# Moving work within the beginnings of two ConvFFN layers, and four smaller moves around them

## The chip, the cores and the metric

The kernel runs on one core of a Trainium2 chip. The metric is the device time of one execution in microseconds (us). Times of a kernel are medians of several executions; the trace is of one execution taken by the hardware profiler. The engines are PE (TensorE, matrix products), PEld (its weight loads), DVE (VectorE), ACT (ScalarE), POOL (GpSimd) and SP (SyncE, which issues DMAs). Each engine works through its own list of instructions in order, and waits on semaphores for the others.

## The reference

A two-layer sequence encoder over x of 1 x 1024 x 1024 in float32. Both layers add a mixing block and a gated convolutional FFN to the residual h, each behind an RMSNorm:

```python
for layer in range(2):
    if layer == 0:
        h = h + gated_deltanet(rmsnorm(h, a_norm[0]), ...)
    else:
        kv = rmsnorm(h, kv_norm) @ w_kv            # keys and values, once
        h = h + chunk_attention(rmsnorm(h, b_norm[0]), w_q, rel_bias, w_out, kv)
    h = h + conv_ffn(rmsnorm(h, f_norm[layer]), ...)
return rmsnorm(h, final_norm)

def gated_deltanet(xn, ...):
    ...                                            # causal conv, SiLU, chunked delta rule: o
    o = rmsnorm(o, out_norm_w) * silu(z)
    return o @ w_out

def conv_ffn(xn, w_up, conv_w, conv_b, w_down):
    h = causal_dwconv(xn @ w_up, conv_w) + conv_b  # three taps along the sequence
    gate, val = h[..., :2816], h[..., 2816:]
    return (silu(gate) * val) @ w_down
```

The model width is 1024, the sequence 1024 long, the FFN 2 x 2816 wide. Attention has 16 heads of 64 over bands of nine chunks of 64 with a relative bias.

## The kernel before

**Products.** Every large product is done in three passes: both operands are cut into a high part (a rounding to the type fp32r, on ACT) and a low part (operand less high part, on DVE or POOL), and PE multiplies high by high, low by high and high by low. `triple` (and `dense` outside the FFN) issues such three matmuls of 128x128 by 128x512. One activation tile is 128 channels by 1024 positions, worked on in two halves of 512.

**Stages in order.** The gated DeltaNet (layer 0's mixing, about the first 668 us), FFN layer 0, the seam in which h is normed for attention and the first K and Q tiles are made (`two_tiles`, near 1310 to 1350), attention, its output product (`queue_out`), FFN layer 1 (from about 1888), the final norm.

**The order of the work.** In the DeltaNet and in attention, a planner written in the kernel (`Weave`, and `Flow` on top of it) calls generators. Each yields the time at which it wants to go on; the planner keeps estimated engine times (`wv.on("A", 0.62)` books 0.62 on ACT) and lays the instructions out from them. `wv.late` is a list of generators that go on when a slot has been reached. In the FFN the order is a list written out by hand: `step` adds a product of 12 matmuls to `seq`, and `at(i, f, rank)` adds the vector work `f` to step i; within a step, jobs run by rising rank. Where the order isn't given by hand (the vector engines in attention, everything in `two_tiles`), the framework's scheduler sets it.

**The FFN.** Both products use a seven-product scheme on 2x2 blocks. The up-projection of the pair j (one `gate` and one `val` tile of 128 channels) takes products (j, n), n from 1 to 7; pair 0 is done in plain by eight steps. For each product the operand is a combination `r` of weight blocks, cut into `uh` (ACT) and `ul` (POOL, in the beginning partly DVE). When a product is done, `after(j, n)` combines its PSUM bank `pu` with `keep` into the pre-activations `vpre` and `gpre`. `taps(j, v, i)` applies tap i of the convolution (v = 1 for `val`, 0 for `gate`; tap 0 with the bias on ACT, L1553; taps 1 and 2 on DVE, L1556), `silu` runs on ACT (L1559), `gated` multiplies on DVE. The down-projection takes two pairs at a time: group g has second products ("d", g, n) with weight operands `dh`, `dl` from `a`, `ay` and activation operands `eh`, `el` from `val`, into banks `pd`, which `drain` copies or adds into `stage` tiles and `send` sends to DRAM. The `when` table says at which step and rank the taps, SiLU and multiply of each pair stand. Helper lines seen in the profile: L1428 is every DVE and POOL addition or subtraction in the FFN, L1449 every rounding on ACT, L1461 to L1463 the three matmuls of `triple`, L1786 the copies of `drain`.

**Norms at the seams.** `norm_steps` sums squares (`nacc`, L401 and L409), sums over partitions with eight tiny matmuls into `pss` (L412), takes the square root (ACT) and reciprocal `rsn` (DVE, L415), broadcasts it with matmuls into `psb` (L425), multiplies h by it (L430, L432) and cuts the result (`xh`, `xl`, L421). It is a generator; the caller places its two sets of matmuls among its own by `next(tail)`. In `two_tiles` and in `plain` of FFN layer 1 these places are given by a pair (i, k): product i, triple k. In `queue_out`, `rest(0)` is put into `wv.late` with `t0 + 11`.

**The other two places.** `yz(k, s)` at the end of the DeltaNet loads y and z tiles, waits until `wv.T + 5.0`, and computes y * SiLU(z) (L1115), which `split_yt` cuts. `split_act` cuts the attention's outputs into `xh` (ACT) and `xl` (L381, even k on DVE, odd k on POOL).

Of the kernel before, what the change touches and what calls it, by code (L numbers as in the profile page):

```python
# [28 lines left out]
def trunk_kernel(  # L29
# [348 lines left out]

    def split_act(dst, src, s, k):
        nc.scalar.copy(dst[0][k][s], src)  # L380
        (nc.vector if k % 2 == 0 else nc.gpsimd).tensor_tensor(dst[1][k][s], src, dst[0][k][s].bitcast(F32), op=ALU.subtract)  # L381

    rsn = const.tile([P, 2, 8], F32, name="rsn")

# [57 lines left out]
    def queue_out(w, h, n, soon, d_r, residual, early, start_need, late_need, g, alloc, begin, begin_need, both, delay, own, ahead):  # L442
# [69 lines left out]
        def rest(s):  # L512
            w_ = 1024 // (KT - n)
            it = norm_steps(h, s, g, normed, keep=True)
            for c in range(KT - n):
                if s == 0:
                    hold.append(load_w(w, c * w_, k0=n, nk=KT - n, w=w_, into=own()))
                wt = hold[c]
                for m in range(c * w_ // P, (c + 1) * w_ // P):
                    ps = alloc()  # L520
                    dense(ps, wt, m * P - c * w_, *acts, [(k - n, k) for k in range(n, KT)], s)
                    yield
                    nc.vector.tensor_tensor(h[m][:, hs(s)], ps, h[m][:, hs(s)], op=ALU.add)
                    nc.scalar.dma_start(out=quarter(d_r, m, s), in_=h[m][:, hs(s)])
                    next(it)

            if s == 1:
                tails.append(it)
                return

            def go():
                t0 = wv.now
                next(it)
                yield
                wv.late.append((lambda: True, lambda: t0 + 3, it))

            t0 = wv.now
            wv.late.append((lambda: True, lambda: t0 + 11, go()))

        tails, hold = [], []  # L540
        acts, normed = [[[[None, None] for _ in range(KT)] for _ in range(2)] for _ in range(2)]
# [29 lines left out]
    with ExitStack() as ph:  # L571
# [535 lines left out]
        def yz(k, s):  # L1107

            yield from wait(("turned", k, s), ("z", k, s))
            yt = yield from take()  # L1110
            nc.sync.dma_start(out=yt, in_=d_y[k][s])
            zt = yield from take()
            nc.sync.dma_start(out=zt, in_=d_z[k][s])
            yield wv.T + 5.0
            nc.scalar.activation(zt, zt, AF.Silu)  # L1115
            yield wv.on("A", 0.62) - wv.slack
            nc.vector.tensor_tensor(yt, yt, zt, op=ALU.mult)
            room.append(zt)
            yield wv.on("D", 0.85) - wv.slack
            yield from wait(("acts", s))  # L1120
            yield from split_yt(yt, s, k)
            room.append(yt)
# [280 lines left out]
    def two_tiles(wts, tail):  # L1403

        pss = [[pacc.tile([P, HALF], F32, name="acc", tag="u", bufs=4) for _ in range(2)] for _ in wts]
        for s in range(2):
            for n, (ps, wt) in enumerate(zip(pss, wts)):
                for i in range(KT):
                    dense(ps[s], wt, 0, xh, xl, FULL[i : i + 1], s, first=i == 0, last=i == KT - 1)
                    if (n, i) in ((0, 6), (1, 3)):  # L1410
                        next(tail, None)
            for _ in tail:
                pass
            yield pss
# [8 lines left out]
    def ffn(layer, h, hp, xs, tail, d_r, last):  # L1423
# [19 lines left out]
        def at(i, f, rank=1):  # L1443

            jobs.setdefault(max(i, 0), []).append((rank, f))
# [169 lines left out]
        def plain(i):  # L1615
            def f():
                s, r, c = ((0, 0, 0), (0, 0, 1), (0, 1, 0), (0, 1, 1), (1, 0, 0), (1, 1, 0), (1, 0, 1), (1, 1, 1))[i]
                if c == 0:
                    first_ps[s, r] = pacc.tile([P, HALF], F32, name="pu0", tag="u", bufs=4)
                if i == 4:  # L1620
                    X[3] = own(hi4, 1)
                x_ = own((lo4, hi4)[c], s)
                for k in range(4):
                    triple(first_ps[s, r], ops0[r, c], x_[k], kc[k], c == 0 and k == 0, c == 1 and k == 3)
                    if (i, k) == ((0, 3), (1, 3))[layer]:
                        next(tail)
                    if (i, k) == ((1, 1), (2, 2))[layer]:
                        for _ in tail:
                            pass
            return f  # L1630
# [8 lines left out]
        for c, (j, n) in enumerate(plan):  # L1639
# [1 line left out]
            due[len(seq)] = (j, n)  # L1641
            step((j, -n), lambda j=j, n=n: product(j, n))
            for g in range(NG):
                for n, o in zip(ORDER, (2, 3, 5, 6, 8, 9, 11) if g == 0 else (-2, 0, 2, 4, 6, 8, 10)):
                    if c == 7 * (2 * g + 1) + 6 + o:
                        step(("d", g, n), lambda g=g, n=n: second(g, n))
        end, fin_at = pos[FP - 1, 7], pos["d", NG - 1, 4]
        early = pos["p", 1, 3]
        for i, (j, n) in due.items():
# [8 lines left out]
                if j > 3 and n in (6, 4):  # L1658
                    at(i - 2, lambda j=j, n=n: left_sum(j, n - 1), 1.05)
            if n != 2 or j > 2:  # L1660
                at(i + 1, lambda j=j, n=n: after(j, n), 0)

        def nx(j, s):
            return pos[j + 1, s] if j + 1 < FP else end + s
# [24 lines left out]
        for j in range(3, FP - 1):  # L1689
# [2 lines left out]

        v0, v1, v2, g0, g1, g2 = [(v, i) for v in (1, 0) for i in range(3)]
        when = {
            0: [(11, (g0,), 0), (12, (v0,), 0), (13, (v1,), 2), (13, (v2,), 2.7), (15, (g1, g2, silu), 2), (17, (gated,), 2)],
            1: [(18, (v0, v1), 2), (19, (v2, g0), 2), (20, (g1,), 2), (21, (g2, silu), 2), (22, (gated,), 2)],
            2: [(24, (v0, v1), 2), (25, (v2, g0), 2), (26, (g1,), 2), (27, (g2, silu), 2), (28, (gated,), 2)],
        }
        for j in range(3, FP - 1):
            late_ = 1 if j == FP - 2 else 0  # L1700
# [722 lines left out]
```

## Time and profile before

| | |
|---|---|
| Time, three executions | 2567.0, 2568.01, 2568.25 us (median 2568.01) |
| Profiled execution | 2567.06 us, its span 2565.4 us |
| PE busy | 2502.9 us (98%), 13933 matmuls |
| DVE / ACT / POOL busy | 1856.2 / 1416.0 / 1468.9 us |
| HBM traffic | 126 GB/s over the span |

The span runs from the first to the last instruction of the profile; about 1.7 us of the execution lie around it. Busy shares are averages over all stages. In rows of the timeline the columns are the start and the duration in us, engine, line, operation, output and inputs with their shape, the count of instructions taken together, and in brackets the idle time before and what ended it. In lists of waits they are total us, times and the longest. In windows the granted clock of PE stands as a share of full speed behind the engines' busy times, then the DMA share and GB/s.

### The profile page before, as it was taken

What the parts mean: (1) busy time and instruction counts of PE and PEld (TensorE: products, weight loads), DVE (VectorE), ACT (ScalarE), POOL (GpSimd) and SP (SyncE); (2) the same over time, 40 slices, a digit from 0 to 9 for tenths busy, and PEclk for the clock granted to TensorE, in tenths of its full rate; (3) what the DMA queues carried; (4) which work ended last, traced back from release to release, by engine and by line L of the source; (5) the groups of instructions that cost most, each with busy time, mean ns of one, the idle gap of its engine ahead of it and who ended that gap; (6) DMA issues with size and microseconds to landing.
All of it is one profiled execution on the core that took longest, in us unless ns stands there. A gap on an engine that the chain in (4) does not pass through costs nothing.

```text
span 2565.4 us, 39382 instructions
## 1 busy us (share of the span) xinstructions
PE 2502.9 (98%) x13933; PEld 2070.2 (81%) x13933; DVE 1856.2 (72%) x3103; ACT 1416.0 (55%) x2736; POOL 1468.9 (57%) x1466
## 2 busy tenths in 40 slices
PE   7999999999999999999999999999999999999998
PEld 5878888888877888888778888887876788888877
DVE  5775874554688888888876666666488788888886
ACT  6444555474455655565555565565455655556544
POOL 3655553445347777777736444443433777777770
PEclk9999999999999999999999999999999999999999
DMA  4533445555337777777932111113332467677795
GB/s 128 137 110 114 128 124 152 147 176 159 101 86 145 147 146 155 155 145 159 204 124 63 54 55 54 52 47 97 107 95 78 135 145 150 143 155 154 152 190 201
DMA packets 320598, 325.15 MB, mean 127 GB/s; under 512 B 32912, under 2 KB 244624, under 8 KB 320400
## 3 DMA queue, kind: packets, MB, share of 16 engines
q1 hardware_dynamic: 289440, 219.33, 28.9%
q0 software_dynamic: 25920, 94.38, 20.8%
q10 hardware_dynamic: 5040, 8.91, 1.0%
q8 instruction: 110, 1.80, 0.3%
q14 instruction: 88, 0.72, 0.1%
HBM read 179.89 MB, written 142.67 MB: 126 GB/s over the span
## 4 chain that ended last, share of the span: by engine, by line
PE 55%; DVE 6%; POOL 4%; issue 3%; ACT 2%; DMA 0%; ACTq 0%; POOLq 0%; DVEq 0%
PE pu L1463 8%; PE pu L1462 8%; PE pu L1461 8%; PE pd L1463 4%; PE pd L1461 4%; PE pd L1462 4%; PE acc L119 3%; PE acc L120 3%; PE acc L121 3%; POOL ul L1428 2%; PE ptp L2139 2%; PE poT L2169 1%; PE sc L2111 1%; PE poT L2168 1%; PE sc L2112 1%
## 5 line engine op out<-in xcount | busy, mean ns | idle before, releaser
L1428 POOL TENSOR_TENSOR ul<-r,uh 128x512 fp32r<-128x512 f32 x282 | 443.0, 1591 | 303.3 <-ACT uh L1449 289.1
L119 PE MATMUL acc<-xh,whi 128*128 128x512 f32 x896 | 373.3, 417 | 1.9 <-DVE kq L686 1.6
L120 PE MATMUL acc<-xl,whi 128*128 128x512 f32 x896 | 353.5, 394 | 1.6 <-POOL xl L421 1.0
L121 PE MATMUL acc<-xh,wlo 128*128 128x512 f32 x896 | 352.8, 394 | 1.1 <-POOL wlo L104 1.1
L1449 ACT CAST uh<-r 128x512 fp32r<-128x512 f32 x296 | 181.7, 623 | 218.4 <-DVE r L1428 169.0
L104 POOL TENSOR_TENSOR wlo<-wraw,whi 128x256 fp32r<-128x256 f32 (+2 forms) x206 | 170.1, 855 | 144.7 <-ACT whi L102 120.7
L1461 PE MATMUL pu<-xh,uh 128*128 128x512 f32 x552 | 216.3, 392 | 1.5 <-DVE h L1329 0.9
L1463 PE MATMUL pu<-xh,ul 128*128 128x512 f32 x552 | 216.1, 391 | 1.1 <-POOL ul L1428 1.0
L1462 PE MATMUL pu<-xl,uh 128*128 128x512 f32 x552 | 215.9, 391 | 1.0 <-POOL xl L421 1.0
L1786 ACT COPY stage<-pd 128x1024 f32<-128x1024 f32 x180 | 174.8, 1013 | 49.2 <-PE pd L1463 49.2
L121 PEld LDWEIGHTS acc<-xh,wlo 128*128 128x128 f32 x896 | 168.7, 188 | 38.7 <-POOL wlo L104 1.6
L120 PEld LDWEIGHTS acc<-xl,whi 128*128 128x128 f32 x896 | 170.1, 190 | 25.7 <-POOL xl L421 3.1
L119 PEld LDWEIGHTS acc<-xh,whi 128*128 128x128 f32 x896 | 169.7, 189 | 24.2 <-DVE kq L686 2.0
L2119 POOL TENSOR_SCALAR sS<-sS,st 128x640 f32<-128x640 f32 (+4 forms) x128 | 85.2, 668 | 171.7 <-DVE st L2118 127.5
L1556 DVE SCALAR_TENSOR_TENSOR val<-vpre,colt,val 128x1023 f32<-128x1023 f32 (+2 forms) x92 | 150.5, 1636 | 40.5 <-ACT val L1553 40.4
L1428 POOL TENSOR_TENSOR dl<-a,dh 128x512 fp32r<-128x512 f32 x90 | 154.8, 1720 | 38.5 <-ACT dh L1449 38.5
L1556 DVE SCALAR_TENSOR_TENSOR gate<-gpre,colt,gate 128x1023 f32<-128x1023 f32 (+2 forms) x92 | 173.0, 1881 | 0.8
L1428 DVE TENSOR_TENSOR r<-r,r 128x512 f32<-128x512 f32 x168 | 133.8, 797 | 29.3 <-POOL ul L1428 28.0
L2117 ACT ACTIVATE sS<-sS,st 128x640 f32<-128x640 f32 (+4 forms) x128 | 89.3, 697 | 100.9 <-DVE st L2116 98.8
L1463 PEld LDWEIGHTS pu<-xh,ul 128*128 128x128 f32 x552 | 104.1, 189 | 24.6 <-POOL ul L1428 3.2
L1461 PEld LDWEIGHTS pu<-xh,uh 128*128 128x128 f32 x552 | 104.1, 189 | 23.6 <-issue 1.3
L1462 PEld LDWEIGHTS pu<-xl,uh 128*128 128x128 f32 x552 | 104.1, 189 | 23.5 <-POOL xl L421 2.1
(405 smaller groups left out, 7146.6 us busy)
## 6 DMA issues: line engine op xcount, KB each, us to landing
r<-in_f_w_up_dram SPq DMA_DIRECT2D x176, 256.0 KB, 4.4
d_r<-stage POOLq DMA_DIRECT2D x78, 512.0 KB, 7.6
d_c<-stage POOLq DMA_DIRECT2D x70, 512.0 KB, 8.0
a<-in_f_w_down_dram SPq DMA_DIRECT2D x72, 256.0 KB, 3.0
wraw<-in_a_w_in_dram SPq DMA_DIRECT2D x32, 512.0 KB, 4.5
d_e<-stage POOLq DMA_DIRECT2D x32, 512.0 KB, 8.8
wraw<-in_a_w_out_dram SPq DMA_DIRECT2D x16, 512.0 KB, 4.3
d_r<-h ACTq DMA_DIRECT2D x32, 256.0 KB, 3.7
```

Of the source, the lines that this page charges most:

```text
L104: nc.gpsimd.tensor_tensor(lo[:, c], raw[:, c], hi[:, c].bitcast(F32), op=ALU.subtract)
L119: mm(ps, hi[:, kw, wcol : wcol + P], rh[k][s], start=st, stop=False)
L120: mm(ps, hi[:, kw, wcol : wcol + P], rl[k][s], start=False, stop=False)
L121: mm(ps, lo[:, kw, wcol : wcol + P], rh[k][s], start=False, stop=sp)
L1428: tt = lambda eng, o, a, b, op: eng.tensor_tensor(o, a, b, op=op)
L1449: copy(hi, src)
L1461: mm(ps, w[0][:, cw], x[0], start=first, stop=False, skip_group_check=True)
L1462: mm(ps, w[0][:, cw], x[1], start=False, stop=False, skip_group_check=True)
L1463: mm(ps, w[1][:, cw], x[0], start=False, stop=last, skip_group_check=True)
L1556: nc.vector.scalar_tensor_tensor(t_[:, a:c1], p_[:, a - step : c1 - step], w[:, 2 - step : 3 - step], t_[:, a:c1], op0=ALU.mult, op1=ALU.add)
L1786: nc.scalar.copy(t_, ps)
L2117: nc.scalar.activation(S, S, AF.Exp, bias=st[:, 1:2], accum_out=st[:, 2:3])
```

## The change

Five groups of edits:

- `split_act`: the low parts of k below 6 all on DVE (before, odd k on POOL).
- `queue_out`: `rest(0)` goes on at slot `t0 + 12` instead of `t0 + 11`.
- `yz`: the wait behind the loads is 8.0 instead of 5.0 of the planner's us.
- The places of the norm's matmuls: in `two_tiles` (1, 1) and (1, 5) instead of (0, 6) and (1, 3); in `plain` of FFN layer 1 (2, 1) and (2, 3) instead of (1, 3) and (2, 2).
- FFN, both layers: the seven second products of group 0 stand at offsets 2, 4, 6, 7, 9, 10, 11 instead of 2, 3, 5, 6, 8, 9, 11, in the order n = 1, 2, 5, 3, 6, 7, 4. In steps: 24, 27, 30, 32, 35, 37, 39 instead of 24, 26, 29, 31, 34, 36, 39. The products (3, 5), (3, 4), (3, 3), (4, 7) and (4, 6) stand one step earlier for it; the rest stay. In `when`, the taps of pairs 0, 1 and 2 are spread, SiLU stands in a step of its own at rank 1.6, and `gated` comes later. `after(3, 2)` stands two steps behind its product instead of one.

```diff
 def split_act(dst, src, s, k):
     nc.scalar.copy(dst[0][k][s], src)
-    (nc.vector if k % 2 == 0 else nc.gpsimd).tensor_tensor(dst[1][k][s], ...)
+    (nc.vector if k % 2 == 0 or k < 6 else nc.gpsimd).tensor_tensor(dst[1][k][s], ...)
...
-            wv.late.append((lambda: True, lambda: t0 + 11, go()))
+            wv.late.append((lambda: True, lambda: t0 + 12, go()))
...
-            yield wv.T + 5.0
+            yield wv.T + 8.0
             nc.scalar.activation(zt, zt, AF.Silu)
...
-                    if (n, i) in ((0, 6), (1, 3)):
+                    if (n, i) in ((1, 1), (1, 5)):
                         next(tail, None)
...
-                    if (i, k) == ((0, 3), (1, 3))[layer]:
+                    if (i, k) == ((0, 3), (2, 1))[layer]:
                         next(tail)
-                    if (i, k) == ((1, 1), (2, 2))[layer]:
+                    if (i, k) == ((1, 1), (2, 3))[layer]:
                         for _ in tail:
                             pass
...
-                for n, o in zip(ORDER, (2, 3, 5, 6, 8, 9, 11) if g == 0 else (-2, 0, 2, 4, 6, 8, 10)):
+                for n, o in zip(ORDER, (2, 4, 6, 7, 9, 10, 11) if g == 0 else (-2, 0, 2, 4, 6, 8, 10)):
...
-                at(i + 1, lambda j=j, n=n: after(j, n), 0)
+                at(i + (2 if (j, n) == (3, 2) else 1), lambda j=j, n=n: after(j, n), 0)
...
-            0: [(11, (g0,), 0), (12, (v0,), 0), (13, (v1,), 2), (13, (v2,), 2.7), (15, (g1, g2, silu), 2), (17, (gated,), 2)],
-            1: [(18, (v0, v1), 2), (19, (v2, g0), 2), (20, (g1,), 2), (21, (g2, silu), 2), (22, (gated,), 2)],
-            2: [(24, (v0, v1), 2), (25, (v2, g0), 2), (26, (g1,), 2), (27, (g2, silu), 2), (28, (gated,), 2)],
+            0: [(11, (g0,), 0), (12, (v0,), 0), (13, (v1,), 2), (13, (v2,), 2.7), (15, (g1,), 2), (16, (g2,), 2), (17, (silu,), 1.6), (19, (gated,), 1.9)],
+            1: [(18, (v0,), 2), (19, (v1,), 2), (19, (v2, g0), 2.1), (21, (g1,), 2), (22, (g2,), 2), (23, (silu,), 1.6), (24, (gated,), 1.1)],
+            2: [(24, (v0, v1), 2), (25, (v2, g0), 2), (27, (g1,), 2), (29, (g2,), 2), (30, (silu,), 1.6), (31, (gated,), 1.9)],
```

More of the change, by code (lines that the diff above doesn't have):

```diff
@@ L380, in split_act @@
         nc.scalar.copy(dst[0][k][s], src)
-        (nc.vector if k % 2 == 0 else nc.gpsimd).tensor_tensor(dst[1][k][s], src, dst[0][k][s].bitcast(F32), op=ALU.subtract)
+        (nc.vector if k % 2 == 0 or k < 6 else nc.gpsimd).tensor_tensor(dst[1][k][s], src, dst[0][k][s].bitcast(F32), op=ALU.subtract)
     rsn = const.tile([P, 2, 8], F32, name="rsn")
```

## The prediction

> **What bounds the kernel now.** I read the page's busy times first, then the waits of PE, then windows over the stretches that the change touches, then the timeline around each wait. Three views carry the argument: the busy line, the waits of PE, and the windows.
>
> ```profile
> PE 2502.9 (98%) x13933; PEld 2070.2 (81%) x13933; DVE 1856.2 (72%) x3103; ACT 1416.0 (55%) x2736; POOL 1468.9 (57%) x1466
> ...
> PE pu L1463 <- POOL ul L1428: 9.7, 17, 1.7
> PE sc L2111 <- DVE st L2115: 6.5, 8, 2.3
> PE pm L939 <- ACT X L932: 2.9, 1, 2.9
> PE pss L412 <- DVE nacc L409: 2.6, 3, 1.4
> ...
> PE pu L1462 <- POOL xl L421: 1.0, 2, 0.7
> ```
> ```profile
> 711.21:781.20 69.99, 64.23 (x269) 49.23 (x268) 58.00 (x59) 37.42 (x52) 38.30 (x26) 1.00 0.34 91
> ...
> 1931.00:2001.00 70.00, 64.48 (x264) 49.48 (x264) 56.40 (x64) 37.84 (x54) 29.08 (x20) 0.98 0.24 79
> ...
> 1000.00:1070.00 70.00, 69.95 (x309) 57.61 (x308) 59.16 (x58) 41.46 (x60) 53.09 (x41) 1.00 0.74 151
> ...
> 551.40:554.70 3.30, 3.30 (x22) 2.97 (x22) 2.70 (x5) 2.79 (x7) 1.78 (x2) 0.50 0.75 251
> 1753.00:1756.00 3.00, 3.00 (x10) 2.32 (x9) 1.53 (x6) 2.05 (x6) 2.05 (x2) 0.50 0.50 151
> 1896.20:1899.50 3.30, 3.30 (x9) 2.63 (x10) 0.20 (x1) 0.74 (x2) 0.11 (x1) 0.50 0.84 235
> 1950.80:1954.10 3.30, 3.30 (x9) 2.55 (x9) 1.68 (x1) 0.05 (x1) 2.89 (x2) 0.50 0.01 3
> ```
>
> PE is busy 98% of the span: 62.5 us of it (2565.4 less 2502.9) are idle, and only PE time can be won. The windows' columns are the stretch, its length, busy time and instructions of PE, PEld, DVE, ACT, POOL, then the granted clock. In the steady FFN stretch (1000 to 1070) PE starts 309 matmuls in 70 us, one every 0.2265 us. In the first seventy us of the two FFN layers, where the down-projection's first group sets in, it starts 269 and 264: 40 and 45 fewer, so 9.1 and 10.2 us of each stretch are lost to idle time, restarts and clock. And four stretches of about 3.4 us run at a granted clock of 0.50: matmuls there are twice as long, so each costs about 1.7 us, after PE had stood idle. In layer 0 the equal stall of 1.74 us left the clock at full speed, so a stall of this size decides it only by where it lies.
>
> **The change, part by part.** Its own time is 2567.06 us (span 2565.4 and 1.66 around it); the median of the runs shown, 2568.01, is 0.95 above it. I sum against 2567.06 and add 0.95 at the end.
>
> *A-layer tail: the gated `z` tiles wait 8.0 instead of 5.0 before SiLU.*
>
> ```profile
> 547.69 0.63 ACT L1115 ACTIVATE spare<-spare 128x512 f32<-128x512 f32 x1 [3.04 <-DMA spare<-d_z]
> 548.34 0.74 ACT L932 COPY X<-pm 32x256 f32<-32x256 f32 x2
> ...
> 549.13 0.21 PE L939 MATMUL pm<-X,D 32*32 32x32 f32 x1 [2.95 <-ACT X L932]
> ...
> PE pu L1461 <- DVE h L1329: 0.9, 1, 0.9
> ...
> PE pu L970 <- DVE vv L847: 0.3, 1, 0.3
> ```
>
> ACT stood 3.04 us in front of a SiLU whose `z` was still on its way from DRAM, with the two copies behind it that PE waited for: 2.95 us idle. The order of the changed program has these copies ahead of that SiLU. The wait goes (2.95), and with it most likely the half-clock stretch at 551 (1.7): 4.6 at best. Against it, the planner lays the rest of the tail out anew (dense products move into the solve, SiLU and its multiply come later), and the later `z` tiles have less room before the output product that reads them; the waits left elsewhere between 480 and 700 are 0.3 to 0.9 each, so a new one costs up to 0.9; with the clock still lost and the stall replaced by four of them, it would end near +1. Range −4.6 to +1; I take −3.5, near the row whose wait is directly undone.
>
> *Attention's end: the first six low parts all on DVE.*
>
> ```profile
> 1746.15 0.42 DVE L2056 CAST qA<-qA 64x512 fp32r<-64x512 f32 x1
> ...
> 1746.94 1.68 DVE L381 TENSOR_TENSOR xl<-eo,xh 128x512 fp32r<-128x512 f32 x1
> ...
> 1749.36 1.51 DVE L2056 CAST qA<-qA 64x512 fp32r<-64x512 f32 x1
> ...
> 1752.25 0.68 DVE L381 TENSOR_TENSOR xl<-eo,xh 128x512 fp32r<-128x512 f32 x1
> ...
> 1746.79 1.29 POOL L381 TENSOR_TENSOR xl<-eo,xh 128x512 fp32r<-128x512 f32 x1 [0.81 <-ACT xh L380]
> 1748.37 2.22 POOL L104 TENSOR_TENSOR wlo<-wraw,whi 128x896 fp32r<-128x896 f32 x1 [0.29 <-ACT whi L102]
> ...
> 1752.13 0.42 PE L2111 MATMUL sc<-kA,qA 128*128 128x320 f32 x1 [2.33 <-DVE st L2115]
> ```
>
> PE waits 2.33 us for the row maximum on DVE, which was late because its subtraction took 1.68 beside POOL's 1.29 (alone 0.68, at 1752.25), and its cast 1.51 beside POOL's 2.22 (alone 0.42, at 1746.15). Without POOL's subtraction the first is 1.0 shorter, so up to 1.0 of the 2.33 goes, and perhaps the half clock behind it (1.7). The three POOL subtractions of each half, 1.29 each, become 0.68 each on DVE: 4.1 us more on an engine that PE waits for here, less about 2.1 of contention. Range −4 to +2; I take −1.5, since the weight-cutting 2.22 stays.
>
> *Norm tail, one slot later (12 for 11).* From 1860 to 1906 PE's waits for `nacc` are these two:
>
> ```profile
> PE pss L412 <- DVE nacc L409: 2.0, 2, 1.4
> ```
>
> 1.37 of it belong to the FFN seam below, the other 0.6 to this tail. A slot is longer, so it goes; the tail then has a slot less to hide. −0.5 (−0.6 to +0.3).
>
> *FFN layer 1's seam: the sums' product moves from after (1,3) to after (2,1), the broadcast from (2,2) to (2,3).*
>
> ```profile
> 1893.61 1.57 DVE L409 TENSOR_TENSOR nacc<-nacc,spare 128x512 f32<-128x512 f32 x1
> ...
> 1895.24 1.06 PE L412 MATMUL pss<-ones,nacc 128*128 128x2 f32 x8 [1.37 <-DVE nacc L409]
> ...
> 1900.98 4.04 DVE L432 SCALAR_TENSOR_TENSOR h<-h,colt,psb 128x512 f32<-128x512 f32 x6 [4.14 <-PE psb L425]
> ```
>
> Six matmuls now stand ahead of `pss`: 6 × 0.2265 = 1.36 us, against 1.37 idle. That wait goes, and with it perhaps the half clock at 1896 (1.7). Six matmuls, not nine, lie between `pss` and the broadcast, so DVE's six `h` products begin 2.4 us earlier if the clock holds and 1.2 if not; PE, 3.1 or 1.4 earlier, then waits up to 0.7 more for the `xl` behind them (the 1.0 of the waits above). Range −2.4 to −1.1; I take −1.8.
>
> *Seam of the two first attention tiles: broadcast from the place behind (1,3) to (1,5), sums from (0,6) to (1,1).*
>
> ```profile
> 1335.40 0.61 PE L425 MATMUL psb<-ident,rsn 128*128 128x128 f32 x4
> ...
> 1337.02 0.61 PE L425 MATMUL psb<-ident,rsn 128*128 128x128 f32 x4
> ...
> 1337.66 1.89 DVE L430 TENSOR_TENSOR nt<-psb,h 128x512 f32<-128x512 f32 x3 [2.77 <-PE psb L425]
> ```
>
> This stretch is ordered by the scheduler, not by hand: in the changed order `pss` lies where it lay, so that half does nothing, and all of `psb` lies five matmuls later (5 × 0.2265 = 1.13). DVE stood 2.77 for it, and PE waits behind DVE and POOL at the end of this seam already. No PE wait that it removes is in the trace. +1.2 (0 to +1.4).
>
> *FFN, both layers: first tiles' taps one per step, SiLU behind the roundings, second products of group 0 two steps apart.*
>
> ```profile
> 715.59 3.50 DVE L1556 SCALAR_TENSOR_TENSOR gate<-gpre,colt,gate 128x1023 f32<-128x1023 f32 x2
> ...
> 753.99 2.59 DVE L1556 SCALAR_TENSOR_TENSOR gate<-gpre,colt,gate 128x1023 f32<-128x1023 f32 x2
> ...
> 716.42 1.28 ACT L1559 ACT_TABLE_LOAD   x1
> 719.11 1.06 ACT L1559 ACTIVATE gate<-gate 128x1024 f32<-128x1024 f32 x1 [1.41 <-DVE gate L1556]
> 720.08 0.60 ACT L1449 CAST uh<-r 128x512 fp32r<-128x512 f32 x1
> ...
> 716.48 1.52 POOL L1428 TENSOR_TENSOR ul<-r,uh 128x512 fp32r<-128x512 f32 x1 [35.60 <-ACT uh L1449]
> 720.81 3.58 POOL L1428 TENSOR_TENSOR ul<-r,uh 128x512 fp32r<-128x512 f32 x2 [2.81 <-DMA r<-in_f_w_up_dram]
> ...
> 723.20 0.50 PE L1463 MATMUL pu<-xt2h,ul 128*128 128x512 f32 x1 [1.74 <-POOL ul L1428]
> ```
>
> The page names a DMA before POOL's 720.81, but what came last is ACT's rounding of 720.08, which stood behind the SiLU of 719.11, which stood 1.41 for a gate tap. With SiLU two steps later the rounding can go 1.41 + 1.06 = 2.5 us earlier, and the 1.74 us stall on `ul` closes: about −2 a layer with the slow restart. In layer 1 the half clock at 1950 follows the same stall (−1.7 if it goes). One step more for five of the second products gives their operands 2.72 us (12 × 0.2265) more, and the remaining 7 us of each layer's 9.1 and more could shrink: I put −5 a layer as the optimistic end. Against it, what is moved later comes due with something else: the table load of 1.28 now stands right in front of the first SiLU, behind which uh for step 20 waits (0.8 by my hand schedule); the multiply of tile 0 and tile 1's taps stand ahead of the weight sums of step 22 (1.5); SiLU of tile 2 at step 30 stands ahead of two drains and a rounding (2 at each of steps 33 and 34), and at step 39 the stage sum stands behind a tap (1.9). These are estimates by hand: the jobs of each step laid end to end at the rows' durations (1.3 a tap, 0.60 a rounding, 1.52 an `ul`, 1.06 a SiLU), DVE and POOL never at the same time. So laid out, it ends at +1.3 a layer: won by step 33, lost by 39. A DVE tap beside POOL took 3.50 for two, 2.59 without, so they do share, but not always. I take −2 in layer 0 and −3 in layer 1 (half of its 1.7 and a little more), range −5 to +1.3 each, −6.7 in layer 1 with the clock.
>
> Sum: −3.5 − 1.5 − 0.5 + 1.2 − 1.8 − 2 − 3 = −11.1; 2567.06 − 11.1 + 0.95 = 2556.9, say 2557. About 5.1 us (0.2%) is what a measurement of this kernel can tell from no change.
>
> **The rivals.**
>
> *The port of DVE and POOL bounds the first group.* Then moving taps and SiLU frees nothing there: each layer gains 2 at step 18 and gives 2 back behind it. Sum without the FFN's 5: −6.1, so 2561.9 (its own range 2559 to 2566). For it: 3.50 against 2.59 for two taps, 2.22 on POOL beside 1.51 for a cast of 0.42. Against it: the steady stretch has DVE 59.16 and POOL 53.09 busy in 70 us, more than the 58.00 and 38.30 of the first group, and PE runs full there. So it is the order, not the load, that costs. The Trainium skill ("Trainium Architecture — The Big Picture", What this means for kernel authors) says that DVE and GpSimd contend for one shared port pair by an exclusive lock, not by splitting the bandwidth; the stretched taps agree, and by that rule the FFN terms would be near 0.
>
> *The clock follows the stalls.* All four half-clock stretches go, and the FFN waits shrink by 4 and 2.8: A tail −4.6, attention −2.5, norm −0.5, tiles' seam +1.2, FFN seam −2.4, layer 0 −4, layer 1 −2.8 − 1.7: −17.3 together, so 2550.7. For it: each of the four rows lies right behind a stall that the change works on. Against it: 0.50 is granted in fixed steps of time, and any new stall of 1.5 us or more can bring it back. The skill ("TensorE: Matmul & The Clock Gate", HAM oscillation) gives the rule as no PE-idle gaps over about 3.4 us; here idle gaps of 1.37 and 2.33 were already followed by 0.50, so the rows speak against that limit, and by it none of the 1.7 could be won by closing such gaps.
>
> *Slower: the first group's drains fall behind.* If DVE, with its taps now one per step through steps 15 to 31, gets more than a step (2.72 us) behind by step 24, every `ul` and stage sum of steps 24 to 40 comes late: eight matmuls that each wait 1.74, as the one at 723.20 did, in place of the 7.1 us lost there besides it (9.1 − 2): 8 × 1.74 − 7.1 = +6.8 a layer, less 2 a layer at step 18, less 6.1 elsewhere, and one more half-clock stretch of 1.7 in layer 0: 13.6 − 4 − 6.1 + 1.7 = +5.2, so 2573. For it: DVE is 58.00 of 70 busy there. Against it: the same work in the same stretch, only later by one or two steps.
>
> That the edit does nothing can be held for the first half of the seam edit alone; elsewhere the order on the engines moves.
>
> **How the numbers follow.** Forecast (2557, own range 2552 to 2562) 0.50; port-bound (2562) 0.24; clock and waits all go (2551) 0.16; drains behind (2573) 0.10. Faster by more than 5.1 us means under 2562.9: nearly all of the first (0.49), half of the second (0.13) and the third (0.16), 0.78. Within: the rest of these, 0.12. Slower: 0.10. The range 2548 to 2566 leaves out the fourth case and the far ends of the others, about 2 in 10.
>
> **What would show it.** After: no half clock near 550 and no 2.95 in front of `pm`; `pss` of layer 1 with under 0.3 idle; no 1.74 at step 18; the first seventy us of the FFN layers with 275 to 285 matmuls instead of 269 and 264. The first of the seam's windows (1310 to 1350 before) about 1 us longer. Wrong it would be if the two FFN windows start no more matmuls than before, or if new waits of 2 us for stage sums or roundings stand at steps 33 to 39.

## The result, and the profile after

The changed kernel takes 2570.6 us (median of 22 executions, 2566.76 to 2574.0), the kernel before 2566.65 (22 executions beside it). The ratio is 1.0016, 95% interval 1.001 to 1.0022: about 4 us slower, where 11 us faster was forecast. The profiled execution took 2569.26 us, its span is 2567.6, so it lies 1.3 us under the median.

First the page's busy line of the changed kernel, then its list of PE's waits (total us, times, longest):

```profile
PE 2500.8 (97%) x13933; PEld 2066.0 (80%) x13933; DVE 1866.3 (73%) x3109; ACT 1415.3 (55%) x2736; POOL 1465.1 (57%) x1460
```
```profile
PE pu L1463 <- POOL ul L1428: 9.7, 20, 1.5
PE pd L1461 <- ACT stage L1786: 5.5, 2, 2.8
PE sc L2111 <- DVE st L2115: 4.0, 8, 0.9
PE pd L1461 <- DVE stage L1428: 3.3, 2, 1.7
...
PE pc L993 <- DVE S L1012: 2.0, 2, 1.6
...
PE ptp L2139 <- DVE pTl L2150: 1.8, 1, 1.8
```

The waits of 2.9 (`pm`), 2.3 (`sc`) and 1.4 (`pss`) are gone as meant, and `ul` still costs 9.7. Second products (`pd`) now wait 5.5 us for the copies of `drain` on ACT (no such wait before) and 3.3 for its sums on DVE (0.4 before), once each in each FFN layer. Windows over the FFN's beginnings and over the one half-clock stretch that stands there now:

```profile
711.21:781.20 69.99, 63.70 (x263) 49.20 (x262) 57.71 (x57) 38.32 (x54) 40.01 (x26) 0.98 0.31 83
1931.00:2001.00 70.00, 62.07 (x261) 47.56 (x260) 58.50 (x63) 37.76 (x53) 29.27 (x19) 1.00 0.26 83
...
762.50:766.00 3.50, 3.50 (x10) 2.74 (x10) 1.25 (x3) 2.23 (x3) 1.28 (x1) 0.54 0.19 54
```

263 and 261 matmuls start in the two windows, against 269 and 264 before: the prediction named that as its refutation. The FFN's matmuls come in the written order, twelve to a step, so the start of every step can be read off the PE timeline of each run. Differences of such starts give the time of each stage in us:

| stage | before | changed | all FFN edits undone (e1) | last variant (e12) |
|---|---|---|---|---|
| start to FFN layer 0 (the DeltaNet) | 667.68 | 665.09 | 671.94 | 668.52 |
| layer 0, steps 13 to 48 | 106.94 | 111.50 | 108.24 | 106.92 |
| end of layer 0 to layer 1 (attention) | 562.20 | 561.63 | 561.84 | 560.84 |
| layer 1, plain products (norm's seam) | 28.48 | 26.62 | 26.58 | 26.60 |
| layer 1, steps 13 to 48 | 107.56 | 109.67 | 106.44 | 104.98 |

A row such as "steps 13 to 48" runs from the start of the first step named to the start of the last. The first row also varies from one execution to the next (below), so each profiled execution is read by stage and not by its sum. The FFN's loss is 4.6 us in layer 0 (5.3 to the layer's last matmul) and 2.1 in layer 1. Both depend on where the clock happened to fall in the kernel before. With its FFN order, layer 0 took 106.9 us in two traces (before, e12) and 108.0 to 108.2 in three (e1, e9, e10), where the stall at step 18 was followed by a half-clock stretch; in layer 1 that stretch is in the 107.56 of the trace before and not in the 106.44 of e1.

In finer stages, each from the start of its first step to the end of its last (a wait in front of a step is counted to the step before):

| steps | layer 0 before | layer 0 changed | layer 1 before | layer 1 changed |
|---|---|---|---|---|
| 13 to 23 | 34.19 | 34.48 | 36.61 | 35.31 |
| 24 to 30 | 22.92 | 19.67 | 22.51 | 19.65 |
| 31 and 32 | 5.74 | 10.09 | 5.76 | 8.57 |
| 33 to 40 | 25.05 | 25.55 | 23.64 | 27.11 |
| 41 to 47 | 19.04 | 21.71 | 19.04 | 19.04 |

So the later second products won some 3 us in steps 24 to 30 of each layer, as meant. The loss lies behind them: at steps 31 and 32 in both layers, at 33 to 40 in layer 1, and at 41 to 47 in layer 0.

At step 31, where the stage copies are late, layer 0 of the changed kernel shows this on PE, ACT, DVE and POOL:

```profile
762.21 0.76 PE L1461 MATMUL pd<-eh,dh 128*128 128x512 f32 x1 [2.75 <-ACT stage L1786]
...
759.71 0.58 ACT L1598 COPY gpre<-pu 128x512 f32<-128x512 f32 x1 [3.32 <-DVE gate L1556]
760.20 1.06 ACT L1559 ACTIVATE gate<-gate 128x1024 f32<-128x1024 f32 x1
761.15 1.92 ACT L1786 COPY stage<-pd 128x1024 f32<-128x1024 f32 x2
...
755.60 1.78 DVE L1428 TENSOR_TENSOR el<-val,eh 128x512 fp32r<-128x512 f32 x1
757.30 2.31 DVE L1556 SCALAR_TENSOR_TENSOR gate<-gpre,colt,gate 128x1022 f32<-128x1022 f32 x1
...
756.79 1.73 POOL L1428 TENSOR_TENSOR dl<-a,dh 128x512 fp32r<-128x512 f32 x1
```

Read from below: the last gate tap of pair 2, moved to step 29, takes 2.31 beside POOL's `dl`. On ACT the next job is the copy into `gpre`, which may not overwrite what that tap still reads: ACT stands 3.32 us. Behind it come SiLU (1.06), and only then the copies of second product 5's banks, to which second product 3 must add. PE stands 2.75. After it the clock is halved (0.54 in the window above), so the one wait costs about 4.6 in layer 0 and 3 in layer 1.

The loss at steps 41 to 47 of layer 0 goes with something else, a send that lands late. Product 6 stands one step later than before, while product 4, whose copies on ACT overwrite the `stage` tiles that product 6's send reads, still stands at step 39. First the changed kernel, then the kernel before:

```profile
782.93 1.76 POOL L1801 DMA_DIRECT2D d_r<-stage  x2
...
792.52 1.01 ACT L1786 COPY stage<-pd 128x1024 f32<-128x1024 f32 x1 [2.07 <-DMA d_r<-stage]
...
796.13 5.86 DVE L1428 TENSOR_TENSOR el<-val,eh 128x512 fp32r<-128x512 f32 x1 [5.54 <-ACT eh L1449]
```
```profile
780.81 1.77 POOL L1801 DMA_DIRECT2D d_r<-stage  x2
...
790.21 1.91 ACT L1786 COPY stage<-pd 128x1024 f32<-128x1024 f32 x2
```

Step 40 begins at about the same time in both (789.48 and 789.81), but the send is issued 2.1 us later, and ACT stands 2.07 for it. The roundings behind the copy come late, POOL's `ul` and `dl` then follow each other without a pause, and a DVE subtraction beside them takes 5.86 us. This wait of ACT on a send, 1.8 to 2.2 us in front of the second copy, and an excess of 2.7 to 4.1 in steps 41 to 47 stand together in layer 0 of five traces (the changed kernel, e2, e4, e7, e11). In the other nine, and in layer 1 of all, where these sends are issued on SP and don't add to what lies in DRAM, neither stands. No run takes away this wait alone, so the cause of these 2.7 us is read from the traces and not shown by an experiment.

### The profile page after: what moved, and what is told of

It reads as the page before. It is cut to its first block, busy times and chain, and to the rows that moved or that the text cites. A ratio compares the mean times of both kernels' runs of the same rounds, so it can differ in the third digit from the quotient of the medians.

```text
span 2567.6 us, 39378 instructions
## 1 busy us (share of the span) xinstructions
PE 2500.8 (97%) x13933; PEld 2066.0 (80%) x13933; DVE 1866.3 (73%) x3109; ACT 1415.3 (55%) x2736; POOL 1465.1 (57%) x1460
## 5 line engine op out<-in xcount | busy, mean ns | idle before, releaser
L1428 DVE TENSOR_TENSOR r<-r,r 128x512 f32<-128x512 f32 x168 | 139.2, 828 | 31.5 <-POOL ul L1428 30.0
L1428 DVE TENSOR_TENSOR el<-val,eh 128x512 fp32r<-128x512 f32 x90 | 87.4, 971 | 49.1 <-ACT eh L1449 49.1
```

Of the source, the lines that this page charges most:

```text
L1428: tt = lambda eng, o, a, b, op: eng.tensor_tensor(o, a, b, op=op)
```

## The experiments

Each was timed beside the kernel before on the same chip; that kernel's medians were 2564.5 to 2566.0. FFN steps are named as in the order of the changed kernel.

**e1: is it the FFN?** All three FFN edits undone.

```diff
-  (2, 4, 6, 7, 9, 10, 11) if g == 0      # offsets, the three rows of `when`,
+  (2, 3, 5, 6, 8, 9, 11) if g == 0       # and after(3, 2), all as before
```

> The changed kernel with its three FFN edits undone (offsets of the second products, the when table, the place of after(3,2)); the norm's places, split_act, the slot of rest(0) and yz stay changed. If the loss is made in the first groups of the FFN layers (the two traces put +5.3 us there in layer 0 and +2.0 in layer 1, and -2.6, -0.6 and -1.9 in the DeltaNet's tail, in attention and in the seam of layer 1), this kernel is about 5 us faster than the one before: 2561 to 2563. If the other four edits lose as well, or only shift what the FFN loses, it is within 2 us of the one before.

2561.69 us against 2565.44: ratio 0.9987 (0.9978 to 0.9996). The four edits outside the FFN gain 3.8 us (about 5 was expected), the FFN's edits lose about 7.5 on top of them (1.0016 less 0.9987 of 2566). Its profiled execution was a late one (2569.06), by the first stage, so only its other rows in the table are used.

**e2, e3, e4: which part, and is it the drain behind SiLU?** Against the changed kernel:

```diff
 e2: when[2] and after(3, 2) as before
+  2: [..., (26, (g1,), 2), (27, (g2, silu), 2), (28, (gated,), 2)]
 e3: the offsets and after(3, 2) as before
+  (2, 3, 5, 6, 8, 9, 11) if g == 0
 e4: SiLU and after(3, 2) behind the drain of product 5
+  2: [..., (27, (g1,), 2), (29, (g2,), 2), (31, (silu,), 1.6), (32, (gated,), 1.9)]
+  at(i + 3, ...after(3, 2), 0.5)
```

In e3 two orders are lost that the new offsets keep: second product 2 cuts pair 1 ahead of its multiply, and pair 3's `gpre` is copied ahead of pair 2's last tap. So e3 computes something else, its waits leave those two out, and its time is a hint only.

> The changed kernel with the row of the when table for pair 2 and the place of after(3,2) as before; the new offsets and the new rows for pairs 0 and 1 stay. Theory A (what is late is ACT: the copy of gpre and SiLU of pair 2 stand in front of the drain of second product 5, which product 3 needs): the 2.9 us wait on the stage copy at step 32 goes in both layers, with the half-clock stretch of 1.7 in layer 0; 5 to 7 us faster than the changed kernel, 2564 to 2566. Theory B (the new offsets crowd the second half of the group, or the port that DVE and POOL share is full): within 1.5 us of the changed kernel, with the waits elsewhere in steps 24 to 40.

> The changed kernel with the offsets of the second products and the place of after(3,2) as before; the when table stays changed. Theory B: it gains most of what the first group lost, 4 to 6 us, 2565 to 2567. Theory A: the drain of product 5 now stands a step earlier, in front of SiLU of pair 2 on ACT, so the 2.9 us wait goes here too, but g2 and SiLU of pair 2 come late for nothing else: 4 to 6 us as well. The two differ in the wait at second product 4: 1.7 to 1.9 as in the changed kernel by A (it is the tap's place on DVE), under 0.7 by B.

> The changed kernel with one thing moved: SiLU of pair 2 at step 31 and its multiply at 32 instead of 30 and 31, and after(3,2) (the copy of gpre) at step 31 rank 0.5, so that both stand behind the drain of second product 5 on ACT. Theory A: second product 3 no longer waits 2.9 us in either layer and the half clock in layer 0 goes: 5 to 8 us faster than the changed kernel, 2563 to 2566. Theory B: the wait comes back on other operands of steps 32 to 38, within 1.5 us of the changed kernel.

Measured: e2 2567.99, e3 2561.66, e4 2569.06 (before 2565.44). Layer 0's steps 13 to 48 took 110.92, 107.66 and 110.66; layer 1's 108.29, 106.62 and 108.79. So e2 and e4 win much less than theory A said, and come out as theory B said: within 1.5 us of the changed kernel, with waits elsewhere. From 700 to 820 us, PE's waits in e2, and then in e4:

```profile
PE pd L1461 <- ACT stage L1786: 2.9, 1, 2.9
PE pd L1461 <- DVE stage L1428: 1.5, 1, 1.5
```
```profile
PE pu L1463 <- POOL ul L1428: 5.1, 7, 1.4
PE pd L1461 <- DVE stage L1428: 1.5, 1, 1.5
PE pu L1461 <- ACT uh L1449: 1.3, 1, 1.3
```

In e2 the wait has only moved: with SiLU of pair 2 back at step 27 it now stands in front of the drain of second product 2, which the new offsets put at 28, and product 5, which needs those banks, waits 2.9. In e4 the drain is free, but the tap is still late, the copy of `gpre` and SiLU push ACT's next tap back, and steps 33 and 34 pay: 1.3 for the rounding `uh` of the one and 1.4 for the low part `ul` of the other, with a half-clock stretch (from 769.8) behind it. Theory A as I wrote it (move the SiLU, and the wait goes) fell in both. By its own sign e3 speaks for B: second product 4 waits 0.4 in layer 0 and not at all in layer 1. It gains more than either theory said (8 us by the ratios, 4 to 6 expected), but it lost two waits, so it doesn't separate the two.

**e7: between the two drains.** The sharper form of A: SiLU must have its tap done early and stand behind the drain of product 2 and ahead of that of product 5, which leaves one step.

```diff
-  2: [..., (27, (g1,), 2), (29, (g2,), 2), (30, (silu,), 1.6), (31, (gated,), 1.9)]
+  2: [..., (26, (g1,), 2), (27, (g2,), 2), (28, (silu,), 1.6), (30, (gated,), 1.9)]
+  after(3, 2) one step behind its product
```

> The changed kernel with the row for pair 2 laid between the drains: g1 at step 26, g2 at 27, SiLU at 28 rank 1.6 (behind the drain of second product 2, ahead of that of 5), multiply at 30, after(3,2) one step behind its product. Theory A (a drain on ACT stands behind a SiLU that waits for a tap): the 3 us wait on the stage copy is gone at both second product 5 and second product 3 and does not come back at steps 33 and 34, 3 us a layer and the half clock of layer 0: 5 to 8 us faster than the changed kernel. Theory B (the offsets leave too little time, wherever the SiLU is): at least 2 of the 3 us show up again in waits of steps 25 to 36, and the kernel is within 2 us of the changed one.

2565.26 us against 2566.0 (ratio 0.9995, 0.9986 to 1.0004), where the changed kernel's ratio is 1.0016: some 5 us better, as the sharper A said and more than B allowed. The windows of the two layers:

```profile
711.21:781.20 69.99, 65.08 (x275) 50.25 (x274) 59.99 (x58) 39.45 (x56) 43.43 (x28) 1.00 0.31 83
1931.00:2001.00 70.00, 65.40 (x276) 50.52 (x276) 60.72 (x63) 37.81 (x54) 34.50 (x22) 1.00 0.26 83
```

275 and 276 matmuls instead of 263 and 261, with DVE and POOL busier than in the changed kernel, and the ACT copies are gone from PE's waits there. The stage sum of product 7 still costs 1.5 and 1.8, and in layer 0 steps 41 to 47 still lose 2.9 behind the late send.

**e6, e11: second product 4.** In the changed kernel one product instead of two stands between second products 7 and 4. e6 makes this change alone in the kernel before; e11 takes e7 and moves the last tap of pair 3 behind the sums.

```diff
 e6:
-  (2, 3, 5, 6, 8, 9, 11) if g == 0
+  (2, 3, 5, 6, 8, 10, 11) if g == 0
 e11, on e7:
-  (nx(3, 3), (g2,), 2), (nx(3, 4), (silu,), 1.6)      # steps 36 and 38
+  (38, (g2,), 2), (39, (silu,), 1.6)
```

> The kernel before with one offset changed: second product 7 of group 0 one place later (10 instead of 9), so that one product instead of two stands between it and second product 4, which needs its two stage sums on DVE. Theory C (the drain of product 7 has 2.72 us instead of 5.44, and the sums take 2.3 and stand behind a tap and two keeps): second product 4 waits 1.7 to 1.9 in both layers, against 0.6 and 0 before; 1 to 3 us slower than the kernel before by the trace. Rival: DVE catches up in the step that the tap leaves free, the wait stays under 0.7, and product 7's own wait for el (0.8) goes: up to 1.5 us faster.

> The last variant of the changed kernel (pair 2's SiLU laid between the drains) with one more thing moved: the last gate tap of pair 3 from step 36 to 38, behind the stage sums of second product 7 on DVE, and its SiLU from 38 to 39. If DVE's order is what makes second product 4 wait (1.7 and 1.9 us), this wait falls to under 0.5 in both layers and the kernel gains 2 to 4 us on that variant: 2561.5 to 2563.5. If the time between products 7 and 4 (one product of 2.72 us for two sums of 1.2 and two keeps of 0.7) is too short whatever stands there, 1 us or more of the wait stays and the gain is under 1.5 us.

e6 took 2579.1 us against 2566.0 (ratio 1.0042, 1.0028 to 1.0056): the direction of theory C, but 11 to 13 us where it said 1 to 3. Layer 0 of e6:

```profile
794.40 0.76 PE L1461 MATMUL pd<-eh,dh 128*128 128x512 f32 x1 [5.47 <-DVE stage L1428]
...
784.30 3.83 DVE L1428 TENSOR_TENSOR val<-val 128x512 f32<-128x512 f32 x1
788.89 0.69 DVE L1428 TENSOR_TENSOR el<-val,eh 128x512 fp32r<-128x512 f32 x1 [0.76 <-ACT eh L1449]
789.50 2.30 DVE L1556 SCALAR_TENSOR_TENSOR gate<-gpre,colt,gate 128x1022 f32<-128x1022 f32 x1
791.72 1.40 DVE L1428 TENSOR_TENSOR keep<-pu,keep 128x512 f32<-128x512 f32 x2
793.04 2.34 DVE L1428 TENSOR_TENSOR stage<-pd,stage 128x1024 f32<-128x1024 f32 x2
...
784.39 1.94 POOL L1428 TENSOR_TENSOR ul<-r,uh 128x512 fp32r<-128x512 f32 x1
785.64 1.93 POOL L1428 TENSOR_TENSOR dl<-a,dh 128x512 fp32r<-128x512 f32 x1
```

The two sums are the last of these five rows of DVE. One of these, a subtraction of 0.68 elsewhere, took 3.83 beside two POOL subtractions in a row. In layer 1 the same subtraction took 1.78 and the wait is 3.9, so the stretched job makes about 1.6 of the 5.47, if the layers differ in nothing else, and the queue the rest. Around each of the two waits 6.8 us run at half clock (0.50 over 791.33 to 798.16 and over 2023.54 to 2030.37), which theory C had not counted: steps 38 and 39 of layer 1 took 12.1 us instead of 5.4. Why the wait is 5.5 here and 1.5 in the changed kernel, whose own DVE jobs there are much the same, was not taken apart further.

e11 took 2563.11 against 2565.2 (ratio 0.9993, 0.9984 to 1.0002), which its time doesn't tell from e7's 0.9995. By the traces the sum's wait is gone in both layers; steps 13 to 48 take 1.9 us less in layer 1 and no less in layer 0 (109.06 and 108.97), so the 2 to 4 us expected came in one layer only. Its waits in layer 1 (1905 to 2045 us), where nothing took its place, and in layer 0 (700 to 820), where the drains on ACT did, which themselves stood 1.84 for the send:

```profile
PE pu L1463 <- POOL ul L1428: 3.6, 6, 0.9
...
PE pd L1463 <- POOL el L1428: 0.5, 1, 0.5
```
```profile
PE pd L1461 <- ACT stage L1786: 1.7, 2, 1.2
```

**e5: SiLU behind the roundings, alone.** The kernel before with the new row for pair 0.

```diff
-  0: [..., (15, (g1, g2, silu), 2), (17, (gated,), 2)]
+  0: [..., (15, (g1,), 2), (16, (g2,), 2), (17, (silu,), 1.6), (19, (gated,), 1.9)]
```

> The kernel before with one row of the when table changed: pair 0's taps one per step, its SiLU at step 17 behind the roundings, its multiply at 19; all else as before. If the prediction's step holds (SiLU ahead of the rounding makes the stall at step 18, and nothing of its size follows), steps 17 to 24 of both layers shrink by 2 us and layer 1 loses its half-clock stretch: 2 to 2 + 3.7 us, so 5 us faster than the kernel before, 2560 to 2562. If the wait only moves (table load and SiLU ahead of the rounding for step 20, the multiply ahead of the sum for step 22: 0.9 and 1.3 in the changed kernel's trace), the stall at step 18 goes, steps 17 to 24 end within 0.5 us of the kernel before, and only the half clock of layer 1 is won: 1 to 2 us faster, 2563.5 to 2565.

2570.27 us against 2566.0 (ratio 1.0015): neither forecast, slower. The stall at step 18 goes (steps 17 and 18 take 6.5 instead of 8.7), and a longer one follows:

```profile
729.10 0.76 PE L1461 MATMUL pu<-xt4h,uh 128*128 128x512 f32 x1 [3.19 <-DVE keep L1428]
...
721.82 1.28 ACT L1559 ACT_TABLE_LOAD   x1
723.12 1.06 ACT L1559 ACTIVATE gate<-gate 128x1024 f32<-128x1024 f32 x1
...
725.07 1.24 ACT L1553 ACTIVATE val<-vpre,colt 128x1024 f32<-128x1024 f32 x1
...
726.34 1.28 DVE L1556 SCALAR_TENSOR_TENSOR val<-vpre,colt,val 128x1023 f32<-128x1023 f32 x1 [4.67 <-ACT val L1553]
727.54 1.41 DVE L1428 TENSOR_TENSOR keep<-pu,keep 128x512 f32<-128x512 f32 x2
```

SiLU and the table load in front of it now stand ahead of pair 1's tap 0 on ACT; DVE, whose next job needs that tap, stands 4.67; and the `keep` behind it on DVE is what frees PE's bank. In the changed kernel the new row of pair 1 lets `keep` pass ahead of the tap, so the two rows only work together. Even so, the changed kernel's steps 20 and 22 take 3.6 and 4.0 instead of 2.72, and steps 13 to 22 of layer 0 end 0.3 us later than before: what step 18 wins is given back within four steps.

**e8: the port.** The changed kernel with group 0's seven `dl` on DVE.

```diff
-  aops[g, n] = cut(src, "d")                       # low part on POOL
+  aops[g, n] = cut_high(src, "d")
+  cut_low(src, *aops[g, n], nc.vector if g == 0 else nc.gpsimd)
```

> The changed kernel with the seven low parts dl of group 0 on DVE (0.68 each) instead of POOL (1.28 and up to 1.75 each) in both layers. If the port that DVE and POOL share is the bound of the first group, this frees 7 x 0.6 = 4 us of it a layer: the waits for ul at steps 25 to 37 shrink and the kernel gets 2 to 5 us faster. If DVE's own order is the bound, DVE has 7 x 0.68 = 4.8 us more a layer in a stretch where PE waits behind its taps and stage sums: 3 to 8 us slower, with the waits at second products 3 and 4 longer.

2571.86 against 2566.0 (ratio 1.0024, 1.0016 to 1.0033): 1 to 2 us above the changed kernel, which the intervals don't tell apart from it, and neither the 2 to 5 faster of the port nor the 3 to 8 slower of DVE's order. The beginnings take 112.2 and 113.2 us. PE's waits in layer 1:

```profile
PE pd L1461 <- DVE stage L1428: 3.9, 2, 2.9
PE pu L1463 <- POOL ul L1428: 3.7, 6, 0.9
PE pd L1461 <- ACT stage L1788: 2.5, 2, 2.3
```

The work is less in sum (0.68 for 1.28 each) and lies on DVE: the stage sums wait 3.9 instead of 1.7. If POOL's work or the port bounded the first group, this should have gained there, and steps 33 to 40 take 30.6 and 30.7 instead of 25.6 and 27.1. That speaks for DVE's queue. Behind the group, in steps 41 to 47 of layer 0, e8 has no wait for a send and loses nothing; whether that is POOL's lighter load or the later product 4 isn't separated.

**e9, e10: the edits outside the FFN, in two halves.** Each alone in the kernel before.

```diff
 e9:  yz wv.T + 8.0; plain of layer 1 at (2, 1) and (2, 3)
 e10: split_act, t0 + 12, two_tiles at (1, 1) and (1, 5)
```

> The kernel before with two edits alone: yz waits 8.0 instead of 5.0, and the norm's two places in layer 1's plain products are (2,1) and (2,3). The seam of layer 1 gave 1.9 us in all the traces with that edit, so at least that. The tail: L932's copies stand ahead of the SiLU that waits for z, so the 2.95 us wait of PE goes; but PE waited 1.6 and 2.8 us for its own instructions at about 545 in two of the five traces with that order. If the tail gives what was forecast (3.5), 5 us faster than the kernel before: 2561; if what it saves is taken by that other wait in part of the executions, 2 to 3.5 us faster: 2562.5 to 2564.

> The kernel before with the other three edits alone: split_act's first six low parts on DVE, rest(0) one slot later, the norm's places in the two tiles' seam at (1,1) and (1,5). From the traces of the kernels that have all three: the 2.33 us wait for the row maximum goes to 0.2 but one of 1.6 to 2.4 for pTl on DVE takes its place, the 0.6 us wait for nacc in the norm's tail is unchanged, the seam loses 0.3. So within 1.5 us of the kernel before: 2564.5 to 2567. If the half-clock stretch near 1753 is really won, up to 2.5 us faster.

e9 2563.88 and e10 2564.09 against 2565.2: ratios 0.9997 and 0.9994, each interval holding 1. Neither half is resolved by its time (−1.3 and −1.1 by the medians; 2 to 5 was expected of e9, at most 1.5 or 2.5 of e10); both halves in one kernel, e1, gain 3.8. By the trace, the seam of layer 1 takes 26.6 us in each of the ten kernels with the edit and 28.5 in each of the four without.

**e12: the best parts.** The four edits outside, layer 0's FFN as before, layer 1's as in e11.

```diff
+  ((2, 3, 5, 6, 8, 9, 11), (2, 4, 6, 7, 9, 10, 11))[layer] if g == 0     # rows of `when` likewise
```

> The best parts together: the four edits outside the FFN as in the changed kernel; FFN layer 0 as in the kernel before; FFN layer 1 with the new offsets and rows, pair 2's SiLU between the drains and pair 3's last tap behind the sums of product 7. From the traces: layer 1's steps 13 to 48 took 105.0 us in that variant against 106.4 with the old rows and full clock (107.6 with the half clock), layer 0's took 109.1 against 106.9. So it should be 1 to 2.5 us faster than the kernel with the FFN edits undone (2561.7), 2559 to 2561, some 5 us faster than the kernel before. If the two layers' costs are not their own (what layer 0 leaves late is carried on, or the half clock falls elsewhere), it ties with the kernel with the FFN edits undone, 2561 to 2563.

2561.03 us against 2564.5 (ratio 0.9983, 0.9974 to 0.9992): faster than both kernels, and not distinguishable by its time from e1, where 1 to 2.5 us less was expected. Its layer 1 takes 104.98 us, 1.5 less than with the old rows at full clock, as in the table.

## Why the prediction was wrong, point by point

- **FFN, −2 and −3: the step that failed.** It measured +5.3 and +2.0. Two parts of it were right: the 1.74 at step 18 goes, in both layers, and steps 24 to 30 take some 3 us less. The net was not. I had laid the jobs out by hand and found new waits at steps 20 (0.8), 22 (1.5), 33 and 34 (2 each) and 39 (1.9), +1.3 a layer, and then set that aside. Measured excess over the usual 2.72: 0.9 at step 20, 1.3 at 22, 2.9 at 31, 1.9 at 34 in layer 1 (0.5 in layer 0), 1.7 to 1.9 at 38. So the layout had the first two and the last nearly right; in place of 2 at each of 33 and 34 came 2.9 at 31 and less behind it. What it missed is that ACT's copy of `gpre` must wait for the tap, the half clock behind the new wait in layer 0, and the send behind step 39, where the layout ended: no term of the prediction stands for a buffer that is still being sent.
- **Why I set it aside.** The argument against the port rival was that DVE and POOL are busier in the steady stretch while PE runs full. That holds (e7 is busier on both and faster than the changed kernel), and it shows that the sum of the work isn't the bound. It doesn't show that a given order is good: the queues of DVE and ACT are in order, and a second product needs its drain within one product's 2.72 us.
- **The port rival** (2562) put the FFN's gain at zero. It was right that what step 18 wins is given back behind it; e8 speaks against the port as the bound of the first group. DVE jobs beside POOL's are still stretched, in e6 up to 3.83 for 0.68. The Trainium skill's sentence ("Trainium Architecture — The Big Picture", What this means for kernel authors) on the exclusive lock of the shared DVE and GpSimd port agrees with that row: POOL's two jobs lie within the 3.83 and take 3.2 of it.
- **The slower rival** named the right group, DVE and a half clock in layer 0, but took 6.8 a layer from eight waits. Here two waits on drains in each layer and, by the traces, one on a send in layer 0 carry the loss. That its 2573 came near 2570.6 is luck.
- **DeltaNet's tail, −3.5.** The 2.95 is gone in all ten traces with the edit. In its place stand 1.6 for `S` and mostly 0.8 for `xh`, and PE stood 0.5 to 2.8 us at line 929 with nothing to wait for in the profile in six of the ten, and in none of the four without. The half clock near 551, which the prediction took as most likely gone with the stall, is gone in three of the ten; seven still have one between 546 and 564, as all four without the edit do. The first stage takes 667.4 us on average with the edit and 668.1 without: −0.7, within its own variation of several us. The changed kernel's own trace shows −2.6, but its 665.09 is the shortest of the fourteen: luck. What PE stood for at line 929 is open; the expectation of e9 calls it a wait for its own instructions, which no run shows. The waits of the changed kernel from 520 to 670 us:

```profile
PE pc L993 <- DVE S L1012: 1.6, 1, 1.6
PE pu L1461 <- DVE h L1329: 0.9, 1, 0.9
PE pm L948 <- ACT xh L1125: 0.8, 1, 0.8
```

- **Attention's end, −1.5, and the tiles' seam, +1.2.** The wait for the row maximum fell from 2.33 to 0.24, but a transpose waits 1.81 for `pTl`, which stands on DVE behind two of `split_act`'s subtractions. The stretch with both edits takes 561.2 us on average over ten traces, 561.8 over four without `split_act`: −0.6, against −0.8 forecast with the norm. In that seam PE's waits rose from 1.0 to 1.3, not by 1.1.

```profile
1753.44 0.42 PE L2111 MATMUL sc<-kA,qA 128*128 128x320 f32 x1 [0.24 <-DVE st L2115]
...
1764.61 0.63 PE L2139 MATMUL ptp<-ident,sS 128*128 128x128 f32 x4 [1.81 <-DVE pTl L2150]
...
1762.98 1.28 DVE L381 TENSOR_TENSOR xl<-eo,xh 128x512 fp32r<-128x512 f32 x2
1764.18 0.28 DVE L2150 TENSOR_TENSOR pTl<-ptp,pTh 128x128 fp32r<-128x128 f32 x1
```

- **Norm slot, −0.5.** Nothing: `pss` stands with the same 0.60 idle (1869.44 before, 1871.56 after). A slot later in the planner didn't shorten the wait.
- **Seam of layer 1, −1.8.** −1.86, right in size and by its steps: the idle 1.37 and the half clock went, the wait for `xl` rose by 0.3.
- **Clock.** Half-clock stretches within the work fell from four to two in the profiled execution. One of the two stands behind the new 2.75, the other (near 1766) behind the 1.81 for `pTl`. That the one near 551 didn't come back is luck, as said above. The Trainium skill ("TensorE: Matmul & The Clock Gate", HAM oscillation) puts the limit at idle gaps of about 3.4 us; 0.54 behind a gap of 2.75 again disagrees.

## What to carry to other kernels

When a job is moved later on an in-order engine, list every job that now stands behind it and what each of these frees (a PSUM bank, a buffer to be overwritten, a buffer that is still being sent), and compare that with the time to the next user; a copy that waits to overwrite a buffer is a wait like any other. Carry the list past the stretch that was moved: the 2.7 us that go with the late send were lost behind the first group. If such a layout by hand says that the gain is given back, believe it before an average over a steady stretch. And two edits that only work together (e5) can't be judged by either alone, so a bundle is best split by traces, stage by stage, and not by times that resolve 2 us.

## What was not expected of the hardware

A DVE subtraction of 128x512 that takes 0.68 alone took 3.83 in e6 beside two POOL subtractions that started 0.09 and 1.34 after it, and ended behind both. In the changed kernel one took 5.86 (796.13), beside three POOL subtractions and the issue of four DMAs, and 5.85 to 5.87 in the other four kernels with the late send. And an idle PE of 2.75 us brought 3.4 us of half clock in layer 0 (0.54 in that window), while the same wait in layer 1 left it at full speed (1.00 over 1931 to 2001).
